# Seven products for eight in the second group's down projection, with weight sums made in two places

## The chip, the cores and the metric

One core of a Trainium2 chip runs the whole program. Its engines are TensorE (PE in the profile, with its weight loads as PEld), VectorE (DVE), ScalarE (ACT), GpSimd (POOL) and SyncE (SP), which here only issues transfers. The metric is the device time of one execution in microseconds; the kernel before took 1772.98 us (median of three runs, 1771.45 to 1773.77).

## The reference

A layer of an encoder, for 1024 tokens of a prompt and 32 tokens of a stream, 1056 in all. Of it this case touches the last part:

```python
h = x + jnp.einsum('bld,de->ble', m, w_out)
u = jnp.einsum('bld,df->blf', rmsnorm(h, g_ffn), w_up)
return h + jnp.einsum('blf,fd->bld', jnp.square(jax.nn.relu(u)), w_down)
```

`w_up` is 1024 x 4096, `w_down` 4096 x 1024. Ahead of it stand one input projection, sparse attention with an indexer, a stick-breaking attention and two gated branches.

## The kernel before, in words

**Numbers in two parts.** Each float32 operand of a product is split into a rounded part h (type fp32r) and the remainder l = x - h. A product is three matmuls, h·h, h·l and l·h (`three`). Splitting is a cast on ScalarE and a subtraction on VectorE or GpSimd.

**Groups and units.** Tokens run in two groups: group one is tokens 0 to 511, group two tokens 512 to 1055, as two halves ("chunks") of 272. Weights come as units: a 128x512 tile of DRAM holds four 128x128 blocks, of four row blocks and one column block. `unit` loads it into `wst` (three buffers), ScalarE casts it into `wh`, GpSimd writes `wl` (five pairs, `WB`). Four blocks times three matmuls are the 12 matmuls that a unit gives for one token chunk; they add up in one PSUM bank.

**The FFN.** `ffn_group` runs ups and downs for one group. An up (`go_up`) makes 128 rows of u for the group's tokens, then relu and square, split again into `mh`/`ml`, which hold 8 such rows. A down (`go_down(e, q)`) takes four of them and adds its product to column block e of y; there are 8 x 8 downs. The normalisation's factor, common to a token, is put on at the end (`acc`), and h is added, reloaded from DRAM into `g.h` (`reload`).

**Quads in group two.** Group two's ups work on two row blocks f, f+1 at a time (`go_up_quad`). Weights are seen as two by two blocks (the two row blocks, the two halves of the 1024 inputs), tokens as two halves, and the two by two product of such blocks is made with seven block products in place of eight, from sums of weights and sums of tokens. `quad_units` makes the weights' sums: SP loads one block into `raw`, and GpSimd issues transfers that add another block to it in SBUF. Sums' pairs are `sh`/`sl` (four pairs). The tokens' sums (`g.sums`) are made once, in `out` and `quarters`. Seven products of 12 matmuls are 84, where eight would be 96. Results come out of PSUM by copies (`part`), additions, `square` and the splits; some products add to a bank whose value up to then was copied out. Downs in group two are plain.

**The order of work.** The program records every operation with a rank and a cost by a formula (`Plan.record`, `cost`), and a planner issues, engine by engine, what it finds ready, of lowest rank first: FAST (reading out PSUM), PREP (weights), MAIN, FILL (matmuls), SLOW. All instructions are issued from one line, L410, so the profile is read by tile names. `behind` makes an SP transfer wait for the instruction recorded last. The planner also knows that GpSimd and some VectorE instructions exclude each other. Beside group one's FFN, the attention of the later tokens, those of group two, runs piece by piece (`late`).

Of the kernel before, what the change touches and what calls it, by code (L numbers as in the profile page):

```python
# [9 lines left out]
F32 = mybir.dt.float32  # L10
# [9 lines left out]
D = 1024  # L20
# [398 lines left out]
class Layer:  # L419
# [77 lines left out]
    def run(self):  # L497
# [34 lines left out]
        self.dh = dt([KB, 128, T], "dh")  # L532

# [104 lines left out]
        self.ffn_group(g2)  # L638
# [750 lines left out]
    def quad_units(self, f):  # L1389

        nc, a, w = self.nc, self.a, self.quads
        with nc.rank(PREP):
            src = lambda i, j: a["w_up"][f + i, j]

            def load(*blocks, out=None):
                st = out
                if out is None:
                    st = nc.tile(w, [128, 512], F32, "raw", bufs=10)
                    nc.sync.dma_start(st, src(*blocks[0]))
                    blocks = blocks[1:]  # L1400
                for b in blocks:
                    nc.gpsimd.dma_start(st, src(*b), accum_op=ALU.add)
                return st

            def part(z, pool, tag, bufs, eng):
                h = nc.tile(pool, [128, 512], F32R, tag + "h", bufs=bufs)
                l = nc.tile(pool, [128, 512], F32R, tag + "l", bufs=bufs)
                nc.scalar.copy(h, z)
                eng.tensor_sub(l, z, h.bitcast(F32))
                return h, l  # L1410

            V, G = nc.vector, nc.gpsimd
            z = load((1, 0), (1, 1))
            z3 = load((0, 0), (1, 0))
            a11, a22, a12 = load((0, 0)), load((1, 1)), load((0, 1))
            s1 = part(z, w, "s", 4, V)
            load((0, 0), out=z)
            s2 = part(z, w, "s", 4, V)
            load((0, 1), out=z)
            s3 = part(z3, w, "s", 4, V)  # L1420
            s4 = part(z, w, "s", 4, G)
            p11 = part(a11, self.wpool, "w", WB, G)
            p12 = part(a12, self.wpool, "w", WB, G)
            p22 = part(a22, self.wpool, "w", WB, G)
        return p11, p12, p22, s1, s2, s3, s4

    def square(self, g, ps, uh, ul, sign=1.0):

        nc = self.nc
        r = g.tmp("ru", "pb", 3)  # L1430
# [236 lines left out]
```

## Time and profile before

| | |
|---|---|
| median of the runs | 1772.98 us |
| profiled execution, its own time | 1771.3 us |
| its span in the profile | 1769.5 us |
| TensorE busy, matmuls | 98%, 11394 |
| VectorE, ScalarE, GpSimd busy | 59%, 55%, 59% |
| DMA | 264.53 MB, mean 149 GB/s |
| adding transfers (queue q0) | 16.78 MB |

Times in the profile count from the span's start. Matmuls are pipelined, and their records overlap, so their count in a stretch says more than their busy time. In the profile `pj` is a PSUM bank of an up or of group one, `pd` one of group two's downs; `xh`/`xl` and `gh`/`gl` are tokens or rows of u, `y` the result, `ru` a relu, `part` a copy out of PSUM. Group two's first matmul starts at 1293.59 us; its FFN fills the time from about 1400 us to the end.

### The profile page before, as it was taken

How to read it: one execution, taken by the hardware profiler on the slowest of the kernel's cores; microseconds unless marked ns; L12 is line 12 of the kernel's file. 1: busy time of each engine (PE TensorE's matmuls, PEld its weight loads, DVE VectorE, ACT ScalarE, POOL GpSimd, SP SyncE). 2: the span in 40 equal slices, each digit the busy share in tenths (PEclk: the TensorE clock that was granted, in tenths of full speed). 3: DMA queues.
4: the chain of work that ended last, by engine and by line, in shares of the span. 5: the costliest groups of instructions: out<-in, count | busy, mean ns of one | idle time of the engine just before them, and what ended most of it. 6: DMA issues, size and time to landing. Idle time of an engine off the chain costs nothing.

```text
span 1769.5 us, 32605 instructions
## 1 busy us (share of the span) xinstructions
PE 1741.2 (98%) x11394; PEld 1599.9 (90%) x11394; DVE 1050.6 (59%) x2284; ACT 976.5 (55%) x2153; POOL 1046.0 (59%) x909
## 2 busy tenths in 40 slices
PE   8999999999999999999999999999999999999999
PEld 7999999999889888988888888888899999999998
DVE  7555578999655644888755455222347843444445
ACT  7444598983255776766665555533236654444441
POOL 3623232435366575999864555665759966666555
PEclk9999999999999999999999999999999999999999
DMA  7243451444566668556344453533486576666634
GB/s 255 74 133 117 116 177 59 147 144 143 178 173 169 177 183 228 172 177 179 100 135 127 125 144 96 156 101 96 155 262 191 153 169 150 151 153 156 154 68 137
DMA packets 169908, 264.53 MB, mean 149 GB/s; under 512 B 28944, under 2 KB 58224, under 8 KB 169744
## 3 DMA queue, kind: packets, MB, share of 16 engines
q1 hardware_dynamic: 160096, 245.33, 47.3%
q0 software_dynamic: 9216, 16.78, 5.9%
q8 instruction: 90, 1.47, 0.4%
q14 instruction: 74, 0.61, 0.1%
q10 hardware_dynamic: 432, 0.34, 0.1%
HBM read 207.87 MB, written 54.40 MB: 148 GB/s over the span
## 4 chain that ended last, share of the span: by engine, by line
PE 85%; DMA 4%; POOL 4%; DVE 3%; issue 2%; ACT 1%; SPq 1%; ACTq 0%; POOLq 0%; DVEq 0%
PE pj L410 52%; PE s L410 13%; PE pd L410 11%; PE t L410 5%; PE o L410 5%; POOL wl L410 1%; DMA wst<-w_ba 1%; SPq L410 1%; DVE xl L410 1%; POOL xl L410 1%; POOL pb L410 1%; POOL acc L410 0%; DMA raw<-w_up 0%; DMA wst<-w_g 0%; DMA xt<-x 0%
## 5 line engine op out<-in xcount | busy, mean ns | idle before, releaser
L410 POOL TENSOR_TENSOR wl<-wst,wh 128x512 fp32r<-128x512 f32 x350 | 485.7, 1395 | 357.2 <-ACT wh L410 324.6
L410 PE MATMUL pj<-xh,wh 128*128 128x512 f32 (+1 forms) x1600 | 557.2, 349 | 0.7 <-DVE vt L410 0.3
L410 PE MATMUL pj<-xh,wl 128*128 128x512 f32 (+1 forms) x1600 | 557.5, 349 | 0.0
L410 PE MATMUL pj<-xl,wh 128*128 128x512 f32 (+1 forms) x1600 | 555.9, 348 | 0.1
L410 ACT CAST wh<-wst 128x512 fp32r<-128x512 f32 x350 | 216.9, 621 | 327.9 <-PE pj L410 167.4
L410 PEld LDWEIGHTS pj<-xh,wh 128*128 128x128 f32 x1600 | 300.8, 188 | 34.0 <-ACT xh L410 1.0
L410 PEld LDWEIGHTS pj<-xh,wl 128*128 128x128 f32 x1600 | 300.8, 188 | 32.9
L410 PEld LDWEIGHTS pj<-xl,wh 128*128 128x128 f32 x1600 | 301.0, 188 | 32.7 <-DVE xl L410 0.3
L410 PE MATMUL pd<-xh,wh 128*128 128x272 f32 x512 | 147.9, 289 | 2.1 <-ACT y L410 1.8
L410 PE MATMUL pd<-xl,wh 128*128 128x272 f32 x512 | 147.6, 288 | 0.0
L410 PE MATMUL pd<-xh,wl 128*128 128x272 f32 x512 | 147.6, 288 | 0.0
L410 DVE TENSOR_TENSOR tt<-t,tt 128x512 fp32r<-128x512 f32 (+2 forms) x168 | 100.5, 624 | 48.6 <-ACT tt L410 46.8
L410 DVE TENSOR_TENSOR_SCAN rem<-rem 128x896 f32<-128x896 f32 (+6 forms) x66 | 118.3, 1816 | 10.5 <-ACT rem L410 10.1
L410 ACT ACTIVATE junk<-score,cand 128x384 bf16<-128x384 f32 (+1 forms) x124 | 116.1, 936 | 9.8 <-DVE cand L410 7.8
L410 POOL TENSOR_TENSOR p<-p,rem 128x895 f32<-128x895 f32 (+6 forms) x66 | 100.9, 1541 | 30.3 <-DVE rem L410 25.3
L410 ACT CAST tt<-t 128x512 fp32r<-128x512 f32 (+2 forms) x168 | 84.6, 541 | 39.1 <-PE t L410 35.2
L410 PE MATMUL s<-wl,xh 128*128 128x256 f32 (+1 forms) x360 | 101.8, 286 | 0.2 <-POOL wl L410 0.2
L410 PEld LDWEIGHTS o<-tt,v 128*128 128x128 f32 x640 | 92.7, 188 | 9.5 <-ACT wh L410 0.8
L410 PE MATMUL s<-wh,xh 128*128 128x256 f32 (+1 forms) x360 | 100.3, 286 | 0.9 <-DVE small L410 0.8
L410 PE MATMUL s<-wh,xl 128*128 128x256 f32 (+1 forms) x360 | 100.8, 283 | 0.0
L410 PE MATMUL s<-k,q 128*128 128x384 f32 (+5 forms) x384 | 95.8, 356 | 4.7 <-DMA k<-dk 2.0
L410 PEld LDWEIGHTS pd<-xh,wh 128*128 128x128 f32 x512 | 96.5, 189 | 3.3 <-ACT y L410 2.0
(260 smaller groups left out, 3847.9 us busy)
## 6 DMA issues: line engine op xcount, KB each, us to landing
wst<-w_down SPq DMA_DIRECT2D x128, 256.0 KB, 2.7
raw<-w_up SPq DMA_DIRECT2D x80, 256.0 KB, 3.2
q<-dq SPq DMA_DIRECT2D x64, 256.0 KB, 5.2
wst<-w_up SPq DMA_DIRECT2D x64, 256.0 KB, 2.7
raw<-w_up POOLq DMA_DIRECT2D x64, 256.0 KB, 4.6
k<-dk SPq DMA_DIRECT2D x48, 256.0 KB, 3.5
v<-dv SPq DMA_DIRECT2D x48, 256.0 KB, 3.6
wst<-w_g SPq DMA_DIRECT2D x42, 256.0 KB, 3.4
```

The source lines that it names most:

```text
L410: fn(*args, **kw)
```

## The change

Group two gets an FFN of its own, `ffn_quads`. Ups pair row blocks four apart (f and f+4 of eight), and run four at a time: `up(q, j)` for j = 0 to 3 makes eight row blocks. With every result it keeps differences of the two token halves and of the two row blocks' results (`T1` to `T4`), split like the results. Then four `down(q, i)` take all of it and make, by seven products of 12 matmuls each, what two column blocks over eight row blocks add to y; there are four rounds (quarters) q.

The sums of `w_up` blocks that the ups need are made beforehand in DRAM, during group one's FFN: `weight_sums` is stepped by `tick`, once after an up and once in each round of downs, and for each quarter copies and adds transfers of 1 MB. The ups then load sums like any weights. The sums of `w_down` blocks are made on VectorE, from SBUF to SBUF, in `down_weights`. Both weights are laid out anew in DRAM so that blocks can be found. Loads use nine buffers in turn (`wst`, `raw`, `rb`, `sg`), pairs seven.

```diff
+    def weight_sums(self):
+        nc, a = self.nc, self.a
+        for (w, q), s in self.sums.items():
+            w11, w12, w21, w22 = (a[w][i, 4 * q:4 * q + 4].rearrange("t (a b) c -> (t a) (b c)", b=4) for i in range(4))
+            s1, s2, s3, s4 = s
+            def begin(out, src):
+                with nc.behind():
+                    nc.sync.dma_start(out, src)
+            def add(out, src):
+                nc.gpsimd.dma_start(out, src, accum_op=ALU.add, max_dma_last_dim=8192)
+            begin(s1, w21)
+            begin(s3, w11)
+            yield
+            add(s1, w22)
+            add(s3, w21)
+            yield
+            begin(s2, s1)
+            yield
+            add(s2, w11)
+            yield
+            begin(s4, s2)
+            yield
+            add(s4, w12)
+            yield
+    def tick(self):
+        with self.nc.rank(SLOW):
+            next(self.steps, None)
...
+    def ffn_quads(self, g):
...
+        def up_weights(q, j):
+            w11, w12, _, w22 = (a["w_up"][i, 4 * q + j] for i in range(4))
+            s1, s2, s3, s4 = (
+                z[32 * j:32 * j + 32].rearrange("a (b c) -> (a b) c", c=512) for z in self.sums["w_up", q])
+            for z, eng in zip((w11, s1, s2, s4, s3, w12, w22), (G, V, G, G, V, G, G)):
+                with nc.rank(PREP):
+                    wt = pair(load(z), eng)
+                yield wt
+        def down_weights(q, i):
+            src = [a["w_down"][p, 4 * q + i] for p in range(4)]
+            with nc.rank(PREP):
+                w11 = load(src[0])
+                wt = pair(w11, G)
+            yield wt
+            with nc.rank(PREP):
+                w21, w22 = load(src[2]), load(src[3])
+                z = turn("raw", raws)
+                add(z, w21, w22)
+                wt = pair(z, G)
+            yield wt
+            with nc.rank(PREP):
+                add(z, z, w11)
+                wt = pair(z, V)
+            yield wt
+            with nc.rank(PREP):
+                w12 = load(src[1])
+                add(z, z, w12)
+                wt = pair(z, G)
+            yield wt
+            for z, y, eng in ((w21, w11, V), (w12, None, G), (w22, None, V)):
+                with nc.rank(PREP):
+                    if y is not None:
+                        add(z, z, y)
+                    wt = pair(z, eng)
+                yield wt
...
+        def up(q, j):
...
+            product(next(wt), x[4], px)
+            pw = turn("bank", banks)
+            with nc.rank(FAST):
+                add(pw, px, p5)
+                square(pw, pw, -1.0)
+                parts(U22[j], pw, V)
+                sub(pz, pw, u12)
+                parts(T3[j], pz, V)
+            py = product(next(wt), x[5])
+            with nc.rank(FAST):
+                add(py, py, p1)
+                square(py, py, 1.0)
+                parts(U11[j], py, V)
+                sub(t1, py, u12)
+                parts(T1[j], t1, G)
+                V.scalar_tensor_tensor(t2, t1, -1.0, pw, op0=ALU.mult, op1=ALU.subtract)
+                parts(T2[j], t2, G)
+            product(next(wt), x[6], px)
+            with nc.rank(FAST):
+                square(px, px, -1.0)
+                parts(U21[j], px, V)
+                V.scalar_tensor_tensor(px, t2, -1.0, px, op0=ALU.mult, op1=ALU.subtract)
+                parts(T4[j], px, V)
+        def down(q, i):
...
+            px = product(next(wt), u[0])
+            gather(0, 0, px, 1.0, 0)
+            pz = product(next(wt), u[1])
+            gather(1, 1, pz, -1.0, 0)
+            product(next(wt), u[2], px)
+            gather(0, 1, px, 1.0, 0)
+            product(next(wt), u[3], pz)
+            gather(0, 1, pz, 1.0, 1)
+            product(next(wt), u[4], px)
+            gather(1, 1, px, -1.0, 1)
+            py = product(next(wt), u[5])
+            gather(0, 0, py, 1.0, 1)
+            product(next(wt), u[6], px)
+            gather(1, 0, px, -1.0, 2)
+        for q in range(4):
+            for j in range(4):
+                up(q, j)
+                if q + j == 0:
+                    self.scales(g)
+            if q == 3:
+                self.reload(g)
+            for i in range(4):
+                down(q, i)
...
     def ffn_group(self, g, late=iter(())):
...
             for f in range(4 * q + 1, min(4 * q + 5, 4 * nq)):
                 go_up(f)
+                if f >= 12:
+                    self.tick()
                 beside(2)
...
+                if q >= 3 and e == 3:
+                    self.tick()
                 beside(1)
```

The order moves with it. On GpSimd in FFN one, in the sixth of its eight rounds of downs, before has the remainders of weight units (`wl`) and squares (`ru`) alone:

```order
L410 TENSOR_TENSOR wl_8286<-wst_8284,wh_8285 128x512
L410 TENSOR_TENSOR ru_8267<-ru_8267 128x512
L410 TENSOR_TENSOR wl_8290<-wst_8288,wh_8289 128x512
L410 TENSOR_TENSOR wl_8294<-wst_8292,wh_8293 128x512
L410 TENSOR_TENSOR ru_8275<-ru_8275 128x512
L410 TENSOR_TENSOR wl_8298<-wst_8296,wh_8297 128x512
```

The changed kernel at the same units (numbers are 16 higher; `dw_up20` is the first sum of the third quarter, `dw_up13` the fourth sum of the second):

```order
L410 TENSOR_TENSOR wl_8302<-wst_8300,wh_8301 128x512
L410 TENSOR_TENSOR wl_8306<-wst_8304,wh_8305 128x512
L410 TENSOR_TENSOR ru_8291<-ru_8291 128x512
L410 DMA dw_up20_94<-w_up 128x2048
L410 DMA dw_up13_93<-w_up 128x2048
L410 TENSOR_TENSOR wl_8310<-wst_8308,wh_8309 128x512
L410 TENSOR_TENSOR wl_8314<-wst_8312,wh_8313 128x512
L410 DMA dw_up22_96<-w_up 128x2048
L410 TENSOR_TENSOR wl_8318<-wst_8316,wh_8317 128x512
```

Three adding transfers stand between remainders; each first waits for a copy. On SP the copies stand between the loads of the same units in the same way:

```order
L410 DMA wst_8304<-w_down 128x512
L410 DMA dw_up20_94<-w_up 16x16384
L410 DMA dw_up13_93<-dw_up11_91 16x16384
L410 DMA wst_8308<-w_down 128x512
L410 DMA wst_8312<-w_down 128x512
L410 DMA dw_up22_96<-w_up 16x16384
L410 DMA wst_8316<-w_down 128x512
L410 DMA wst_8320<-w_down 128x512
L410 DMA wst_8324<-w_up 128x512
L410 DMA wst_8327<-w_up 128x512
L410 DMA dw_up21_95<-dw_up20_94 16x16384
```

Before, SP has these loads alone. On VectorE in group two, before has for a round of downs one addition to y for every bank (`pd`), and a remainder of a sum (`sl`) before the next quad:

```order
L410 TENSOR_TENSOR y1_14401<-pd_16306,y1_14401 128x272
L410 TENSOR_TENSOR y1_14401<-pd_16307,y1_14401 128x272
L410 TENSOR_TENSOR y1_14401<-pd_16311,y1_14401 128x272
L410 TENSOR_TENSOR y1_14401<-pd_16312,y1_14401 128x272
L410 TENSOR_TENSOR y1_14401<-pd_16316,y1_14401 128x272
L410 TENSOR_TENSOR y1_14401<-pd_16317,y1_14401 128x272
L410 TENSOR_TENSOR sl_16374<-raw_16368,sh_16373 128x512
```

The changed kernel's downs of the second quarter:

```order
L410 TENSOR_TENSOR wl_16162<-rb_112,wh_16161 128x512
L410 TENSOR_TENSOR sl_16166<-wst_16156,sh_16165 128x512
L410 TENSOR_TENSOR y1_14457<-pj_16155,y1_14457 128x272
L410 TENSOR_TENSOR rb_112<-rb_112 128x512
L410 TENSOR_TENSOR wst_16178<-raw_16176,raw_16177 128x512
L410 TENSOR_TENSOR y1_14457<-y1_14457,pj_16133 128x272
L410 TENSOR_TENSOR y1_14457<-y1_14457,pj_16160 128x272
L410 TENSOR_TENSOR wl_16171<-raw_16157,wh_16170 128x512
L410 TENSOR_TENSOR y1_14457<-pj_16155,y1_14457 128x272
L410 TENSOR_TENSOR raw_16176<-raw_16176,raw_16172 128x512
L410 TENSOR_TENSOR wst_16178<-wst_16178,raw_16172 128x512
L410 TENSOR_TENSOR y1_14457<-pj_16160,y1_14457 128x272
```

Sums of 128x512 from SBUF (`rb`, `wst`, `raw`) and remainders now stand between the additions to y. On TensorE, where the second quarter turns from ups to downs, the first three down products (`pj_16133`, `pd_16139`, `pd_16149`) have run as far as the first three ups allow, and these are the first rows that need the fourth (`xh1`/`xl1` and `uh`/`ul` are the kept results and differences):

```order
L410 MATMUL pj_16133<-xh1_110,wh_16131 128x272
L410 MATMUL pd_16149<-uh_15798,sh_16147 128x272
L410 MATMUL pd_16139<-xh1_110,wh_16137 128x272
L410 MATMUL pj_16133<-xl1_111,wh_16131 128x272
L410 MATMUL pj_16133<-xh1_110,wl_16132 128x272
L410 MATMUL pd_16149<-ul_15799,sh_16147 128x272
L410 MATMUL pd_16149<-uh_15798,sl_16148 128x272
L410 MATMUL pd_16139<-xl1_111,wh_16137 128x272
L410 MATMUL pd_16139<-xh1_110,wl_16138 128x272
L410 MATMUL pj_16155<-xh1_110,wh_16153 128x272
```

Before has no such place: its downs take four rows of u of the round before, while the next ups run between them.

More of the change, by code (lines that the diff above doesn't have):

```diff
@@ L532, in run @@
         self.dh = dt([KB, 128, T], "dh")
+        self.sums = {(w, q): [dt([128, 2048], f"d{w}{q}{i}") for i in range(4)] for w in ("w_up",) for q in range(4)}
+        self.steps = self.weight_sums()
         self.wpool = nc.open("w")
@@ L1387, in quarters @@
             part(3, t4)
[L1389 to L1425, printed above, removed]
@@ new lines, in scales, with reload @@
+    def scales(self, g):
+        nc = self.nc
+        for c in range(len(g.chunks)):
+            ps = self.bank("pj")
+            nc.tensor.matmul(ps[:, :g.n], self.ones, g.acc[c], start=True, stop=True)
+            with nc.rank(FAST):
+                v = g.tmp("rv", "pb", 3)
+                nc.vector.tensor_scalar(v, ps[:, :g.n], 1.0 / D, EPS, op0=ALU.mult, op1=ALU.add)
+                nc.vector.reciprocal(g.acc[c], v)
+    def reload(self, g):
+        with self.nc.rank(PREP):
+            self.nc.sync.dma_start(
+                g.h.bitcast(F32), self.dh[:, :, g.lo:g.lo + g.w].rearrange("e p t -> p e t"))
@@ new lines, in up @@
+            px = product(next(wt), x[0])
+            keep(p1, px)
+            pz = product(next(wt), x[1])
+            keep(p5, pz)
+            product(next(wt), x[2], px)
+            keep(u2, px)
+            product(next(wt), x[3], pz)
+            with nc.rank(FAST):
+                add(pz, pz, u2)
+                square(u12, pz, 1.0)
+            product(next(wt), x[4], px)
[6 more added lines that the diff above has]
+                parts(T3[j], pz, V)
@@ new lines, in ffn_quads, with ffn_group, source, go_up @@
+        for q in range(4):
[3 more added lines that the diff above has]
+                    self.scales(g)
+            if q == 3:
+                self.reload(g)
+            for i in range(4):
+                down(q, i)
+    def ffn_group(self, g, late=iter(())):
+        nc, a = self.nc, self.a
+        nq, us = DFF // 512, {}
+        def source(name, row, col, t):
+            return a[name][2 * row + col, t]
+        def go_up(f):
+            units = [self.unit(source("w_up", f % 8 // 4, j, 4 * (f // 8) + f % 4)) for j in range(2)]
+            us[f] = uh, ul = g.mh[:, f % 8], g.ml[:, f % 8]
+            def done(c, cs, ps):
+                r = g.tmp("ru", "pb", 3)
+                nc.scalar.activation(r, ps, AF.Relu)
+                nc.gpsimd.tensor_mul(r, r, r)
+                nc.scalar.copy(uh[:, cs], r)
+                nc.vector.tensor_sub(ul[:, cs], r, uh.bitcast(F32)[:, cs])
+            self.column_block(units, lambda k, cs: (g.h[:, k, cs], g.l[:, k, cs]), done, g.chunks)
@@ L1511, in go_down @@
         def go_down(e, q):
-            units = [self.unit(a["w_down"][e, q])]
+            units = [self.unit(source("w_down", e % 2, q % 2, 4 * (q // 2) + e // 2))]
             def done(c, cs, ps):
@@ L1610, in _host_arrays @@
     out["w_ba"], out["w_bb"], out["w_out"] = units(f["w_branch_a"]), units(f["w_branch_b"]), units(f["w_out"])
-    out["w_up"], out["w_down"] = units(f["w_up"]), units(f["w_down"])
+    up, down = units(f["w_up"]), units(f["w_down"])
+    out["w_up"] = np.ascontiguousarray(
+        up.reshape(4, 2, 4, 2, 128, 512).transpose(1, 3, 0, 2, 4, 5).reshape(4, 16, 128, 512))
+    out["w_down"] = np.ascontiguousarray(
+        down.reshape(4, 2, 4, 2, 128, 512).transpose(1, 3, 2, 0, 4, 5).reshape(4, 16, 128, 512))
     out["g_mix"] = np.ascontiguousarray(f["g_mix"].reshape(KB, 128).T)
```

203 lines of the change are left out of this document (102 added, 101 removed).

## The prediction

> **What bounds the kernel now.** I read the page first: busy time by engine, the granted clock, and the chain that ended last.
>
> ```profile
> PE 1741.2 (98%) x11394; PEld 1599.9 (90%) x11394; DVE 1050.6 (59%) x2284; ACT 976.5 (55%) x2153; POOL 1046.0 (59%) x909
> PEclk9999999999999999999999999999999999999999
> PE 85%; DMA 4%; POOL 4%; DVE 3%; issue 2%; ACT 1%; SPq 1%; ACTq 0%; POOLq 0%; DVEq 0%
> ```
>
> TensorE is busy nearly throughout, at full clock, and 85% of the chain is its own. Busy matmuls overlap in the records, so I checked by stretches how densely they are issued (columns: PE, PEld, DVE, ACT, POOL busy with counts, clock, DMA share, GB/s).
>
> ```profile
> 1028.00:1275.00 247.00, 247.00 (x1202) 208.63 (x1202) 90.77 (x170) 105.43 (x191) 151.00 (x124) 1.00 0.43 126
> 1310.00:1330.00 20.00, 18.87 (x150) 18.65 (x150) 8.42 (x13) 9.73 (x17) 12.09 (x14) 1.00 0.99 283
> 1400.00:1410.00 10.00, 9.75 (x73) 9.18 (x73) 7.14 (x12) 5.55 (x15) 7.38 (x8) 1.00 0.53 149
> 1410.00:1420.00 10.00, 8.01 (x53) 7.79 (x52) 6.89 (x10) 4.23 (x10) 8.49 (x8) 0.84 0.79 159
> 1420.00:1430.00 10.00, 10.00 (x78) 9.70 (x77) 4.47 (x10) 4.83 (x12) 3.52 (x4) 0.99 0.60 129
> 1430.00:1440.00 10.00, 9.06 (x73) 8.84 (x71) 4.99 (x12) 5.45 (x14) 6.07 (x6) 1.00 0.90 191
> 1440.00:1450.00 10.00, 9.12 (x72) 9.12 (x73) 1.39 (x3) 6.64 (x17) 8.39 (x8) 1.00 0.70 168
> 1500.00:1700.00 200.00, 200.00 (x1597) 200.00 (x1596) 86.40 (x196) 90.02 (x196) 121.22 (x106) 1.00 0.63 143
> ```
>
> From 1500 to 1700, in group two's FFN, some 8 matmuls start per microsecond and nothing waits: that stretch is bound by the number of matmuls. Its price per matmul comes from the chain, whose pieces repeat once for each up quad with four downs (96 + 84 = 180 matmuls of 272 columns):
>
> ```profile
> 1537.27 8.92 PE pj L410 x71
> ...
> 1695.38 8.92 PE pj L410 x71
> ```
>
> Seven repeats in 158.11 us: 158.11 / (7 x 180) = 125.5 ns a matmul.
>
> **The matmuls removed.** Group two's downs are 8 x 8 column blocks x 2 token halves x 4 x 3 = 1536 matmuls; seven products for eight make 1344. The ups keep seven products (1344 matmuls). 192 x 125.5 ns = **-24.1 us**, if TensorE still sets the pace. The rest of the sum asks where it would not.
>
> **Side work in group two.** Durations, by form, from 1510 to 1690:
>
> ```profile
> L410 POOL TENSOR_TENSOR wl<-wst,wh 128x512 fp32r<-128x512 f32 x32 | 41.4, 1298 | 35.4 <-ACT wh L410 34.7
> L410 DVE TENSOR_TENSOR y<-pd,y 128x272 f32<-128x272 f32 x64 | 28.3, 442 | 45.1 <-PE pd L410 45.1
> L410 ACT CAST wh<-wst 128x512 fp32r<-128x512 f32 x32 | 19.9, 620 | 46.0 <-PE pd L410 35.8 <-PE pj L410 7.9 <-POOL wl L410 2.3
> L410 DVE TENSOR_TENSOR sl<-raw,sh 128x512 fp32r<-128x512 f32 x24 | 15.8, 686 | 23.8 <-ACT sh L410 23.8
> L410 DVE SCALAR_TENSOR_TENSOR pj<-pj,ru 128x272 f32<-128x272 f32 x32 | 14.2, 442 | 2.4 <-ACT ru L410 2.4
> L410 DVE TENSOR_TENSOR xl<-pj,xh 128x272 fp32r<-128x272 f32 x32 | 13.9, 434 | 3.3 <-ACT xh L410 3.3
> L410 ACT ACTIVATE ru<-pj 128x272 f32<-128x272 f32 x32 | 12.6, 394 | 13.4 <-DVE pj L410 13.4
> L410 ACT CAST xh<-pj 128x272 fp32r<-128x272 f32 x32 | 12.2, 380 | 0.0
> ```
>
> Either kind of unit is now 84 matmuls, 84 x 125.5 = 10.54 us; each other engine must stay below that.
> An up: ScalarE has 7 weight casts (0.620), 3 copies and 7 casts (0.380), 4 relus (0.394): 9.7 us. VectorE has 2 weight remainders (0.686) and 16 instructions of 272 columns (0.44): 8.4. GpSimd has 5 remainders (1.298) and 2 of 272 columns, at most 0.92 each: 8.3. All fit, ScalarE narrowly. Its 7 loads of 0.262 MB are 174 GB/s, an up and a down together (11) 137: below the 283 reached above, and near the 143 of 1500 to 1700.
> A down: ScalarE 7 x 0.620 = 4.3 (four more copies in the first quarter); GpSimd 4 x 1.298 = 5.2; VectorE 4 sums and 3 remainders of 128x512 from SBUF, 7 x 0.686 = 4.8, and 7 instructions that read out PSUM, 7 x 0.442 = 3.1, in all 7.9. In the last quarter the outputs are finished too: 14 in place of 7, 4.8 + 6.2 = **11.0 us, over 10.54**.
>
> These sums and remainders have two SBUF inputs, and such instructions take longer beside a busy GpSimd (by form, 1360 to 1400; the third row by group, 1150 to 1260):
>
> ```profile
> L410 DVE TENSOR_TENSOR raw<-raw 128x272 f32<-128x272 f32 x4 | 6.1, 1528 | 0.0
> L410 POOL TENSOR_TENSOR wl<-wst,wh 128x512 fp32r<-128x512 f32 x9 | 12.7, 1424 | 0.0
> L410 DVE TENSOR_TENSOR xl<-ru,xh 128x512 fp32r<-128x512 f32 x10 | 14.2, 1425 | 42.5 <-ACT xh L410 42.5
> ```
>
> Against 0.442 from PSUM, 272 columns from SBUF took 1.53; 512 columns took between 0.686 and 1.425. Bounds for one of the seven: 0.686 and 1.425. I take 0.78, near the row of the same stage, since GpSimd is wanted for 5.2 of 10.5 us there (in the 0.686 row's stretch for about 60%). Then the last four downs want 7 x 0.78 + 6.2 = 11.65, that is 4 x 1.1 = 4.4 us more than the matmuls; the other twelve, at 8.6, only read PSUM out late now and then. **+5 us** for the downs (0 to +53, below).
> The Trainium skill, SBUF — State Buffer, "Who interferes with whom", says that a VectorE instruction with two SBUF inputs and a GpSimd instruction that reads SBUF shut each other out for the whole of the first one. The trace agrees where GpSimd never rests (1.53 against 0.442); by that rule a down's 4.8 + 5.2 = 10.0 us would still go into 10.54.
>
> **Start and turns.** The five rows from 1400 to 1450 hold 349 matmuls where 50 / 0.1255 = 398 would fit: 6 us lost as group two's FFN starts. The worst stop:
>
> ```profile
> 1413.82 2.27 DVE L410 TENSOR_TENSOR sl<-raw,sh 128x512 fp32r<-128x512 f32 x1
> 1416.14 0.39 PE L410 MATMUL pj<-gh,sl 128*128 128x272 f32 x1 [1.99 <-DVE sl L410]
> ```
>
> A weight sum's remainder, behind GpSimd, holds TensorE for 2 us, and the clock of that 10 us row falls to 0.84. The changed kernel loads finished sums, with no adding transfer between two remainders; but its ups follow one another, so GpSimd has less room to catch up. Bounds -6 and +3; I take **-2**.
> The Trainium skill, TensorE: Matmul & The Clock Gate, "Why this matters for your kernels", asks for gaps of more than about 3 us before the clock falls. Here 2 us did it; by the page, the second rival below would cost 9 us instead of 15.
> At each of four turns from ups to downs, the first downs need the last up's differences. The order puts nine matmuls each of three down products ahead, then what needs the differences as it comes in; after the last up product 19 matmuls, 2.4 us, stand before its first use. The chain there is relu 0.394, multiply 0.442, cast 0.380, remainder 0.434 = 1.65 us and four handoffs. It fits closely: **+1** (0 to +15).
>
> **The sums' transfers in FFN one.** 16 copies and 16 adding transfers of 128x2048 float32, 1.05 MB each, 16.8 MB of either kind. In the order the first copy stands on SP behind the loads of the first row below, the last copy behind the reload of the second; so they run where before has 1028 to 1275. Prices are from 1500 to 1700:
>
> ```profile
> 1024.62 3.78 SPq L410 DMA_DIRECT2D wst<-w_down  x2
> 1266.59 0.38 SPq L410 DMA_DIRECT2D xh<-dh  x1
> ```
>
> ```profile
> q1 hardware_dynamic: 10821, 19.71, 35.8%
> q0 software_dynamic: 4768, 8.66, 27.0%
> ```
>
> Copies 0.358 x 200 / 19.71 = 3.6 us per MB, adds 0.27 x 200 / 8.66 = 6.2: 61 + 104 = 165 us of all engines. Free is (1 - 0.43) x 247 = 141: 24 us short. By the fastest row (283 GB/s at 0.99), 33.6 MB take 119 and fit. A transfer waits for the one before it, on SP for copies and on GpSimd for adds, and the weight loads, and remainders, of FFN one stand behind it. Their reserve:
>
> ```profile
> ACT wh L410 <- PE pj L410: 47.2, 23, 2.2
> ```
>
> ```profile
> 1195.04 19.31 SPq L410 DMA_DIRECT2D wst<-w_up  x8
> ```
>
> Casts wait for TensorE to free a buffer (1150 to 1260), so all five pairs are full; a unit lasts (19.31 - 0.33) / 7 = 2.7 us, and four pairs ahead, less cast and remainder (1.9), are 8.9 us. So the shortage costs 0 to 15 us. I take **+2**: the new rows are four times as long as those priced.
> Before, GpSimd issued 64 adding transfers in group two; those go, with no gain on TensorE's path.
>
> **Sum.** 1769.5 - 24.1 + 5 - 2 + 1 + 2 = 1751.4 us of span. The profiled execution took 1771.3, 1.8 over its span, and the median 1772.98 is 1.7 over that: 1751.4 + 3.5 = **1755 us**.
>
> **Rivals.**
> *The sums' transfers saturate* (0.14): 24 us short less 8.9 reserve = 15 in place of 2: 1768. For it, 165 against 141; against it, 119.
> *The turns stall* (0.10): the remainder comes 2.3 us late as at 1413.82, with 0.16 x 10 = 1.6 us of lost clock, four times: 15 in place of 1: 1769. Against it, the order's fill.
> *VectorE and GpSimd bind the downs*, slower (0.09): at 1.425 us for each of the seven, a down is 10.0 + 3.1 = 13.1 us, 2.5 over, twelve times, and in the last quarter 16.2, 5.6 over, four times: 30 + 23 = 53 in place of 5: 1803. It decides once the seven average 1.15 us, where the excess (12 x 0.6 + 4 x 3.7 = 22) eats the matmuls saved. For it, the 1.425 row; against it, 0.686 in the same stage.
> *All hidden, the start mended* (0.05): 1769.5 - 24.1 - 6 + 3.5 = 1743.
> That the change doesn't do what it says is excluded: the order has 192 matmuls fewer.
>
> **Chances and range.** The forecast has 0.62, with 1746 to 1763 of its own. The range 1746 to 1770 takes in the first two rivals and leaves out the third and fourth with a little of each tail. The measurement tells 0.2%, 3.5 us, from no change. Faster (below 1769.4): 0.62 + 0.05 + nearly all of 0.14 + half of 0.10 = 0.84; within: 0.08; slower: 0.08.
>
> **What would show it.** Right: 192 fewer matmuls; 125 ns each in the middle of group two; FFN one still at 1202 matmuls in its 247 us. Wrong: TensorE waiting for `wl` in FFN one, with a DMA share near 1 (transfers); waits for VectorE's `ul` or `xl` once per 84 us (turns); VectorE near 100% in the downs with 128x512 sums above 1.1 us (port). The forecast falls if any of these costs over 10 us, or if group one's part before 1028 moves.

## The result, and the profile after

The changed kernel took 1784.9 us (median of seven runs, 1781.0 to 1796.3), the kernel before 1771.45 beside it (seven runs; the 1772.98 above is of three): 1.0088 times as long, 95% interval 1.0071 to 1.0105. It is slower, by 13 us by the medians and 16 by the ratio; 1755 was forecast, and the range ended at 1770. Its runs also lie farther apart than those of before (15 us against 3.4), and the profiled execution, 1796.3, is the slowest of them. So a single stage of it is compared below with the same stage of other kernels.

The page of the changed kernel, busy time, clock and the chain that ended last:

```profile
PE 1740.3 (97%) x11202; PEld 1586.7 (88%) x11202; DVE 1164.0 (65%) x2448; ACT 1015.4 (57%) x2249; POOL 1070.5 (60%) x901
PEclk9999999999999999999999999999999999999999
PE 78%; DMA 8%; DVE 7%; POOL 2%; issue 2%; ACT 1%; SPq 0%; POOLq 0%; DVEq 0%; ACTq 0%
```

192 matmuls are gone (11394 to 11202), but TensorE's share of the chain fell from 85% to 78%, and what came in is DMA (4% to 8%) and VectorE (3% to 7%). The program falls into three stages by places that every kernel here has: the start, VectorE's first remainder `xl<-ru,xh` of FFN one, TensorE's first 272-column matmul of group two, and the end. The stages hold the same work in all of them but a_first, a_all, a_mix and a_mixh, where FFN one has 7 to 88 matmuls more and the stage ahead of it as many fewer. Read from the instructions' starts (us):

| kernel | to FFN one | FFN one | group two | span |
|---|---|---|---|---|
| before | 858.1 | 435.5 | 475.9 | 1769.5 |
| changed | 866.6 | 465.6 | 462.3 | 1794.5 |
| difference | +8.5 | +30.1 | -13.6 | +25.0 |

**FFN one.** The stretch by windows, first of before, then of the changed kernel (PE, PEld, DVE, ACT, POOL busy with counts, clock, DMA share, GB/s):

```profile
1028.00:1180.00 152.00, 152.00 (x783) 129.99 (x783) 65.37 (x143) 74.17 (x138) 90.84 (x75) 1.00 0.45 130
1180.00:1293.00 113.00, 113.00 (x500) 93.55 (x499) 37.69 (x44) 35.62 (x61) 74.47 (x60) 1.00 0.43 130
```

```profile
1028.00:1180.00 152.00, 148.44 (x769) 126.59 (x768) 66.22 (x160) 76.78 (x140) 95.72 (x80) 1.00 0.70 196
1180.00:1293.00 113.00, 102.67 (x420) 80.85 (x419) 20.35 (x24) 28.90 (x50) 59.64 (x52) 0.95 0.90 248
```

From 1180 on 420 matmuls run where 500 did, at a DMA share of 0.90 and a clock of 0.95. The DMA view of 1150 to 1293, before and then changed (queues: packets, MB, share; issues: count, size, median us to landing):

```profile
q1 hardware_dynamic: 9529, 17.56, 40.7%
wst<-w_down SPq DMA_DIRECT2D x25, 256.0 KB, 2.6
wst<-w_up SPq DMA_DIRECT2D x22, 256.0 KB, 2.6
```

```profile
q1 hardware_dynamic: 6958, 23.13, 45.8%
q0 software_dynamic: 1440, 10.49, 37.9%
dw_up<-w_up POOLq DMA_DIRECT2D x11, 1024.0 KB, 12.5
wst<-w_up SPq DMA_DIRECT2D x22, 256.0 KB, 6.5
wst<-w_down SPq DMA_DIRECT2D x21, 256.0 KB, 4.4
```

A weight load that landed in 2.6 us now takes 4.4 to 6.5. In 1150 to 1335, ScalarE's casts, which used to wait for TensorE, wait for the loads:

```profile
ACT wh L410 <- DMA wst<-w_down: 48.8, 9, 10.7
ACT wh L410 <- DMA wst<-w_up: 32.9, 12, 6.1
```

**Group two.** Two windows, the first without a turn, the second around the third quarter's turn from ups to downs:

```profile
1598.00:1640.00 42.00, 42.00 (x336) 42.00 (x336) 25.45 (x54) 25.44 (x58) 26.33 (x22) 1.00 0.56 164
1640.00:1664.00 24.00, 22.62 (x170) 21.47 (x169) 22.84 (x46) 17.02 (x42) 17.37 (x14) 1.00 0.28 82
```

Between turns 8 matmuls start per microsecond, as before. At the turn it is 170 where 191 would fit at 125.5 ns each, 2.7 us lost, and VectorE is busy for 22.84 of 24 us. The chain in the turn's last 7 us runs through VectorE alone (start, length, what):

```profile
1655.82 0.59 DVE wl L410
1656.41 0.36 DVE pd L410
1656.77 1.35 DVE wst L410
...
1661.26 1.03 DVE sl L410
1662.29 0.35 DVE pj L410
1662.64 0.35 DVE y L410
1663.00 0.04 issue
1663.04 9.07 PE pj L410 x70
```

The last up's differences stand in VectorE's queue behind sums (`wst`) and remainders (`wl`, `sl`) of the first downs' weights, and these are long. By form, 1500 to 1780:

```profile
L410 DVE TENSOR_TENSOR wl<-raw,wh 128x512 fp32r<-128x512 f32 x16 | 16.0, 998 | 9.0 <-ACT wh L410 8.8
L410 DVE TENSOR_TENSOR wst<-wst,raw 128x512 f32<-128x512 f32 x10 | 12.1, 1209 | 2.0 <-POOL wl L410 2.0
L410 DVE TENSOR_TENSOR raw<-raw 128x512 f32<-128x512 f32 x9 | 10.4, 1153 | 0.0
```

Over all 138 of the 128x512 kind from 1437 to 1782 the mean is 1.04 us, where I took 0.78.

### The profile page after: what moved, and what is told of

The parts are those of the page before. It is cut to its first block, busy times and chain, and to the rows that moved or that the text cites. A ratio compares the mean times of both kernels' runs of the same rounds, so it can differ in the third digit from the quotient of the medians.

```text
span 1794.5 us, 32622 instructions
## 1 busy us (share of the span) xinstructions
PE 1740.3 (97%) x11202; PEld 1586.7 (88%) x11202; DVE 1164.0 (65%) x2448; ACT 1015.4 (57%) x2249; POOL 1070.5 (60%) x901
## 4 chain that ended last, share of the span: by engine, by line
PE 78%; DMA 8%; DVE 7%; POOL 2%; issue 2%; ACT 1%; SPq 0%; POOLq 0%; DVEq 0%; ACTq 0%
PE pj L410 53%; PE s L410 13%; PE t L410 5%; PE o L410 4%; DMA wst<-w_up 4%; PE pd L410 2%; POOL wl L410 1%; DMA wst<-w_down 1%; DVE pj L410 1%; DMA q<-dq 1%; DVE xl L410 1%; ACT wh L410 1%; DVE wst L410 0%; DVE raw L410 0%; DMA k<-dk 0%
## 5 line engine op out<-in xcount | busy, mean ns | idle before, releaser
L410 PE MATMUL pj<-xh,wh 128*128 128x512 f32 (+1 forms) x1864 | 640.5, 344 | 15.6 <-ACT wh L410 7.1
L410 PE MATMUL pj<-xh,wl 128*128 128x512 f32 (+1 forms) x1864 | 639.7, 344 | 5.2 <-POOL wl L410 5.1
L410 PE MATMUL pj<-xl,wh 128*128 128x512 f32 (+1 forms) x1864 | 636.5, 342 | 0.7 <-DVE xl L410 0.7
L410 PEld LDWEIGHTS pj<-xh,wh 128*128 128x128 f32 x1864 | 354.4, 190 | 54.5 <-ACT wh L410 10.3
L410 PEld LDWEIGHTS pj<-xh,wl 128*128 128x128 f32 x1864 | 353.8, 190 | 42.1 <-POOL wl L410 8.8
L410 PEld LDWEIGHTS pj<-xl,wh 128*128 128x128 f32 x1864 | 354.2, 190 | 34.0 <-DVE xl L410 1.2
L410 DVE TENSOR_TENSOR y<-pj,y 128x512 f32<-128x512 f32 (+1 forms) x95 | 55.5, 584 | 88.7 <-PE pj L410 88.5
L410 PE MATMUL o<-tt,v 128*128 128x256 f32 (+1 forms) x640 | 99.6, 279 | 0.4 <-ACT wh L410 0.4
L410 PE MATMUL t<-ident,p 128*128 128x128 f32 x596 | 90.4, 276 | 2.5 <-POOL p L410 2.5
L410 DVE TENSOR_TENSOR xl<-ru,xh 128x512 fp32r<-128x512 f32 x32 | 36.1, 1127 | 84.0 <-ACT xh L410 83.9
```

The costliest lines, as they stand in the source:

```text
L410: fn(*args, **kw)
```

## The experiments

Eighteen kernels beside the two. The ratio is to the kernel before, run beside them (its medians lay between 1768.3 and 1770.5). The stages are those of the table above, from one profiled execution each.

| kernel | ratio (interval) | to FFN one | FFN one | group two |
|---|---|---|---|---|
| b_sums | 1.0149 (1.0134-1.0164) | 858.1 | 463.1 | 477.7 |
| b_copies | 1.0004 (0.9993-1.0014) | 861.7 | 436.8 | 474.2 |
| a_nosums | 0.9914 (0.9901-0.9927) | 860.3 | 435.5 | 458.0 |
| a_noadds | 0.9975 (0.9960-0.9989) | 857.9 | 459.3 | 447.3 |
| a_norem | 1.0036 (1.0023-1.0049) | 857.5 | 458.2 | 454.0 |
| a_shift | 1.0052 (1.0035-1.0068) | 861.0 | 459.5 | 462.1 |
| a_half | 1.0053 (1.0038-1.0068) | 857.9 | 455.8 | 460.9 |
| a_early | 1.0068 (1.0043-1.0093) | 861.4 | 458.9 | 462.3 |
| a_first | 1.0179 (1.0164-1.0194) | 888.0 | 447.6 | 462.0 |
| a_all | 1.0248 (1.0226-1.0271) | 913.1 | 446.5 | 447.5 |
| a_r5 | 1.0010 (0.9994-1.0027) | 859.8 | 449.5 | 461.2 |
| a_both | 1.0001 (0.9986-1.0016) | 857.5 | 447.4 | 457.0 |
| a_late | 1.0033 (1.0019-1.0048) | 857.1 | 438.3 | 478.2 |
| a_best | 1.0075 (1.0055-1.0095) | 855.9 | 437.2 | 485.0 |
| a_p2k | 1.0056 (1.0035-1.0076) | 861.1 | 455.9 | 461.3 |
| a_p2kr5 | 1.0030 (1.0016-1.0044) | 859.3 | 452.5 | 460.7 |
| a_mix | 1.0130 (1.0116-1.0145) | 893.3 | 438.4 | 460.3 |
| a_mixh | 1.0133 (1.0108-1.0158) | 893.8 | 437.7 | 461.4 |

Two readings of the table itself. Up to FFN one, kernels with the same program there stand at 855.9 to 861.7, so the changed kernel's +8.5 is that execution's own and not the change's. In FFN one, five kernels with the same transfers and buffers (changed, a_shift, a_noadds, a_norem, a_half) took 455.8 to 465.6: that stage varies by 10 us from one execution to the next, and with it the time. Group two repeats within 2 us (460.3 to 462.3 where its program is the same; a_nosums, whose ups load other blocks, has 458.0).

### The transfers, and the sums on VectorE, apart

b_sums is the kernel before with `weight_sums` and its ticks, at the same places:

```diff
                 go_up(f)
+                if f >= 12:
+                    self.tick()
                 beside(2)
...
+                if q >= 3 and e == 3:
+                    self.tick()
                 beside(1)
```

> The kernel before, plus the 16 copies and 16 adding transfers of the changed kernel at the same places of group one's FFN; nothing uses the sums. Theory one (the transfers take the weight loads' turn in the last 170 us of FFN one, where 12 of 16 adds stand): 15 to 28 us more than before, 1787 to 1800, and group two's first 272-column matmul 15 to 30 us later than 1293.6. Rival (the loss has another source: the new layout of DRAM, or the planner's other order): within 4 us of before, as the prediction's +2 had it.

a_nosums is the reverse:

```diff
-        self.steps = self.weight_sums()
+        self.steps = iter(())
...
-            s1, s2, s3, s4 = (
-                z[32 * j:32 * j + 32].rearrange("a (b c) -> (a b) c", c=512) for z in self.sums["w_up", q])
+            s1, s2, s3, s4 = (a["w_up"][i, 4 * q + j] for i in (2, 0, 1, 3))
```

> The changed kernel without the 32 transfers of the sums: the ups load plain blocks of w_up in their place, so u is computed from other weights, by the same number of loads, casts and matmuls. Theory one: 15 to 28 us less than the changed kernel, 1757 to 1770, and FFN one ends as before. Rival (another source): still 1780 to 1790. With theory one and nothing lost elsewhere it would be the prediction less 2, 1753; what it stands above that is the turns'.

The transfers alone added 1.49%, 26 us, to the kernel before; without them the changed kernel is at 0.9914, 31 us below its 1.0088, and FFN one takes 435.5 us, as before. Theory one holds by both: the transfers cost 26 to 31 us, nearly all in FFN one. The window of b_sums reads like that of the changed kernel:

```profile
1180.00:1293.00 113.00, 102.82 (x420) 80.56 (x419) 23.93 (x25) 30.28 (x53) 64.06 (x55) 0.95 0.89 249
```

a_noadds takes VectorE's four sums out of each down:

```diff
-                z = turn("raw", raws)
-                add(z, w21, w22)
-                wt = pair(z, G)
+                wt = pair(w21, G)
...
-                add(z, z, w11)
-                wt = pair(z, V)
+                wt = pair(w22, V)
... (so for the other two)
```

> The changed kernel without the four sums of w_down that VectorE makes for each down: the products take the plain blocks instead, so y is another sum, with the same loads, casts, remainders and matmuls. Theory two (VectorE, with seven two-input instructions of 1.06 us mean in place of 0.78, is behind where ups turn to downs, 13 us in four turns): 8 to 13 us less than the changed kernel, 1772 to 1777. Rival (the turns wait for the last up's own chain of relu, multiply, cast and remainder): within 3 us of the changed kernel.

a_norem leaves VectorE's work and takes GpSimd's:

```diff
+            if eng is None:
+                return h, last[0]
             eng.tensor_sub(l, st, h.bitcast(F32))
+            if eng is V:
+                last[0] = l
...
-                wt = pair(w11, G)
+                wt = pair(w11, None)
... (so for all four G of down_weights)
```

> The changed kernel without GpSimd's four remainders in each down: those products use VectorE's last remainder in their place, so y has wrong low parts; VectorE's instructions stay as they are, all of them. If the two-input instructions are slow because GpSimd holds what both read SBUF through: they fall from 1.06 to 0.6-0.7 us in the downs, and the time falls by 8 to 13 us, to 1772 to 1777, as without the sums. If they are slow by themselves: 1.06 stays, and the time too, 1782 to 1788.

Without the sums group two took 447.3 us, 15.0 less, and the turns' stops are gone (a window around a turn):

```profile
1620.00:1640.00 20.00, 19.83 (x157) 19.47 (x156) 16.07 (x38) 14.62 (x36) 13.81 (x13) 1.00 0.43 131
```

That is 157 matmuls where 159 would fit at 125.5 ns, with VectorE at 16 of 20 us. So the turns waited for VectorE's backlog, not for the last up's own chain. In a_norem, without GpSimd's remainders of the downs, VectorE made all its sums and remainders, and each was shorter (1500 to 1755):

```profile
L410 DVE TENSOR_TENSOR wl<-raw,wh 128x512 fp32r<-128x512 f32 x15 | 11.9, 795 | 8.5 <-ACT wh L410 5.4 <-DMA raw<-w_up 3.1
L410 DVE TENSOR_TENSOR wst<-wst,raw 128x512 f32<-128x512 f32 x8 | 5.5, 684 | 0.0
L410 DVE TENSOR_TENSOR raw<-raw 128x512 f32<-128x512 f32 x7 | 5.4, 767 | 0.0
```

The two kinds of sum shown before fall from 1.15 and 1.21 us to 0.77 and 0.68 (all 128x512 ones: 1.04 to 0.76), and group two gains 8.3 of the 15.0. That TensorE no longer needs GpSimd's remainders is not what gained it: in group two's FFN TensorE waited for GpSimd for 1.7 us in the changed kernel and for 2.2 in a_norem. More than half of what VectorE's sums cost is thus the two engines' standing in each other's way; the rest is their number. The Trainium skill, SBUF — State Buffer, "Who interferes with whom", has GpSimd's reads and VectorE's two-input instructions shut each other out; these rows agree, 1.21 us beside GpSimd's remainders of the downs and 0.68 without them.

a_shift gives VectorE fewer remainders and GpSimd more:

```diff
-            for z, y, eng in ((w21, w11, V), (w12, None, G), (w22, None, V)):
+            for z, y, eng in ((w21, w11, G), (w12, None, G), (w22, None, G)):
```

> The changed kernel with two more of each down's remainders on GpSimd (six) and one left on VectorE beside its four sums. If VectorE's own load decides: 5 x 1.06 + 3.1 = 8.4 us a down, and the time falls by 5 to 10 us, 1775 to 1780. If the time in which the two engines exclude each other decides: what is left of VectorE's instructions grows longer beside GpSimd's 6 x 1.42 us, and the time is within 3 us of the changed kernel's, or longer.

Its group two takes 462.1 us, as before the edit, and the sums left on VectorE grew longer:

```profile
L410 DVE TENSOR_TENSOR wst<-wst,raw 128x512 f32<-128x512 f32 x8 | 9.9, 1237 | 0.0
L410 DVE TENSOR_TENSOR raw<-raw 128x512 f32<-128x512 f32 x7 | 8.9, 1276 | 0.3 <-POOL wl L410 0.3
```

The second reading of its expectation holds: moving such work between the two engines moves nothing. The ratio, 1.0052 for 1.0088, comes from the start and FFN one (861.0 and 459.5 us), where nothing was edited.

a_half makes two of a down's four sums by adding transfers into SBUF:

```diff
-                w21, w22 = load(src[2]), load(src[3])
-                z = turn("raw", raws)
-                add(z, w21, w22)
+                z = load(src[2])
+                G.dma_start(z, src[3], accum_op=ALU.add)
                 wt = pair(z, G)
... (w21 + w11 in the same way)
```

> The changed kernel with two of each down's four sums (w21 + w22 and w21 + w11) made by adding transfers into SBUF, 32 in all, and two left on VectorE. By theory two VectorE has 5 x 1.0 + 3.1 = 8.1 us a down in place of 10.5, and 10 to 15 of the 18.6 us go that the kernel without sums gained: 1769 to 1775. If the adding transfers come too late for the products: within 4 us of the changed kernel, with waits for them at TensorE.

Group two gained 1.4 us, not 10, though VectorE has two instructions fewer in each down; a down also loads five blocks for four now, beside its two adding transfers. TensorE waits for other things (1420 to 1770):

```profile
PE pj L410 <- DVE wl L410: 2.7, 2, 2.3
PE pd L410 <- ACT wh L410: 2.2, 2, 2.0
PE pj L410 <- ACT ut L410: 2.1, 3, 1.2
```

The first two are remainders and casts of weights that came late, the third is a copy of a result. That these waits are what ate the gain is likely, but no run takes them away.

### Why the transfers cost 26 us: place, buffers, kind, pieces

a_early ticks from the third up on; a_first puts two steps behind each projection and gate of the first 450 us; a_all does so too, and goes on through FFN one with w_down's sums, so that VectorE makes none:

```diff
-                if f >= 12:
+                if f >= 2:
                     self.tick()
```

```diff
             self.project_b(p)
+            self.tick()
+            self.tick()
```

```diff
-for w in ("w_up",) for q in range(4)}
+for w in ("w_up", "w_down") for q in range(4)}
...
+            for z, eng in zip((w11, s1, s2, s4, s3, w12, w22), (G, G, V, G, V, G, V)):
+                with nc.rank(PREP):
+                    wt = pair(load(z), eng)
```

> The changed kernel with its transfers one step after each up of FFN one from the third up on, not from the thirteenth: the same 32 transfers, begun some 170 us earlier, most of them beside the attention of group two's tokens, where before has a DMA share of 0.23 to 0.5. Theory one a (they cost because they bunch where FFN one runs alone and takes a weight unit every 2.7 us): most of the 26 us goes, 1758 to 1768. Theory one b (each transfer of a megabyte holds up what is queued behind it, wherever it stands): 20 us or more stay, 1778 to 1788.

> The same 32 transfers, two steps after each projection and gate of the first 450 us, where before has a DMA share of 0.2 to 0.6 and weights are wanted more seldom. Theory one a: 1754 to 1762, near the kernel without the transfers (1755.6). Theory one b: 20 us or more over that, lost before 450 us.

> Both w_up's sums and w_down's by transfers, 64 in all: w_up's in the first 450 us, w_down's from there to the end of FFN one; VectorE makes no sums, and each down loads seven blocks in place of four. Theories one a and two together: the 29 us of the transfers and most of the 18 us of VectorE's sums go, 1738 to 1750. Against: the transfers of w_down beside FFN one cost 5 to 15 of it again (1750 to 1762); one b: above 1775.

None paid. In a_early 825 matmuls run from 860 to 1028 where before has 934, at a share of 0.70:

```profile
860.00:1028.00 168.00, 155.52 (x825) 133.85 (x825) 84.85 (x162) 89.24 (x173) 103.33 (x76) 0.95 0.70 197
975.00:995.00 20.00, 9.39 (x51) 7.64 (x49) 6.60 (x19) 5.19 (x10) 6.26 (x6) 0.80 1.04 244
```

Of TensorE's two longest stops there, 5.7 and 4.9 us, the second is a wait for a load of the attention's own (`q`). The second row shows what the average of 0.70 hides: adding transfers are under way up to 990, the share is 1.04 (packets count where they start, so it can pass 1), and 51 matmuls run where before has 114. a_first lost 42 us, 30 of it by the table before FFN one. The 12 that the table has in FFN one are work that the planner moved there: that stage holds 2315 matmuls for 2227 in before, and TensorE's waits in it come to 0.2 us. That the transfers bunch in FFN one is then not the whole cause: stretches that are free by their averaged share have no room while an adding transfer is under way. a_all's group two, 447.5 us, is that of a_noadds: with w_down's sums made elsewhere it is short, but the 64 transfers cost 66 us before group two (55.0 and 11.0), where a_first's 32 cost 42.

a_r5 lets loads in FFN one use two halves of the tile `rb` beside `wst`'s three buffers; a_both adds a_half's edit:

```diff
+            self.loads += 1
+            i = self.loads % 5 - 3
+            if self.wide and i >= 0:
+                st = self.rb[:, 512 * i:512 * i + 512]
+            else:
                 st = nc.tile(self.wpool, [128, 512], F32, "wst", bufs=3)
```

> The changed kernel with five buffers for weight loads in FFN one in place of three (the two more are halves of a tile that FFN one leaves idle); transfers and sums as they are. With three buffers a load may take about 3 x 2.7 us less cast and remainder (1.9), some 6.2 us, before TensorE waits; with five some 11.7. Theory (the loads' longer way beside the transfers, 5.2 to 6.5 us median in FFN one's last 170 us for 2.6 before, is what TensorE waits for): 10 to 22 us less than the changed kernel's ratio, 1762 to 1774. Rival (the 16 DMA engines are full, and no reserve helps what lasts 150 us): within 6 us, 1778 to 1786.

> Both edits: the sum of what each of the two gains, 1748 to 1762, below the kernel before (1769) if either theory holds in full; near the better of the two if the same time is counted twice.

Five buffers brought the ratio to 1.0010, 14 us less, and FFN one to 449.5 us, though its loads landed no sooner (1150 to 1293):

```profile
q0 software_dynamic: 1584, 11.54, 40.9%
wst<-w_up SPq DMA_DIRECT2D x14, 256.0 KB, 7.5
wst<-w_down SPq DMA_DIRECT2D x13, 256.0 KB, 7.0
```

So half of the transfers' price was the loads' longer way through three buffers: at one unit per 2.7 us, three bear 3 x 2.7 - 1.9 = 6.2 us by this estimate, and the loads of `w_up` took 6.5. Some 14 us in FFN one stayed. a_both, 1.0001, equals the kernel before and no more.

What stayed was still open, and the copies were set apart from the adding transfers: b_copies drops the adds of b_sums, and a_late moves half of all steps into group two.

```diff
             def add(out, src):
-                nc.gpsimd.dma_start(out, src, accum_op=ALU.add, max_dma_last_dim=8192)
+                return
```

```diff
-                if f >= 12:
+                if f >= 12 and f % 3 == 0:
                     self.tick()
...
-        for _ in self.steps:
-            pass
... (a tick after each up and down of ffn_quads)
```

> The kernel before with the 16 copies alone, without the 16 adding transfers. By their time on the engines (copies 3.0 us a megabyte, adding transfers 5.2): 16.8 x 3.0 = 50 of 138 us, and a cost of 9 of the 26 us or less, 1769 to 1778. If what counts is that loads queue behind copies, which use the same queue as the loads while the adding transfers have one of their own: 15 us or more, 1784 and up.

> The changed kernel with the transfers of quarters zero and one in FFN one, spread over the same stretch, and those of quarters two and three in group two's FFN, one step after each up and down of its first two quarters. If full DMA engines are the price: FFN one, with 8 of 16 adding transfers, loses 5 to 12 us in place of 22 to 28, group two has room (share 0.3 to 0.6, nine buffers), and the time is 10 to 18 us less than the changed kernel's, 1767 to 1775. If each transfer has its price wherever it stands: within 4 us of the changed kernel.

> The transfers spread so, five load buffers in FFN one, and two of each down's four sums by adding transfers. If full engines are the price: below the 1.000 of the two edits without the spreading by 5 to 10 us, 1758 to 1765, faster than before by 0.3 to 0.6%. If not, or if the adding transfers of the downs and those of w_up get into each other's way in group two: 1768 to 1776.

The copies cost nothing that can be measured (1.0004); loads beside them land in 2.6 to 2.8 us, though they share a queue. Their window, and that of a_late with 5 adding transfers in place of 11:

```profile
1180.00:1293.00 113.00, 113.00 (x500) 93.62 (x499) 35.71 (x41) 36.99 (x64) 76.29 (x62) 1.00 0.58 198
```

```profile
1180.00:1293.00 113.00, 113.00 (x500) 93.55 (x500) 36.81 (x44) 35.15 (x60) 75.94 (x63) 1.00 0.65 191
```

Both keep TensorE's 500 matmuls; at 0.89 and above it is 420 to 456. The prices follow: adding transfers 0.379 x 143 / 10.49 = 5.2 us of all engines per MB, copies, from b_copies' queue row less that of before, 2.3:

```profile
q1 hardware_dynamic: 9727, 27.96, 57.7%
```

(0.577 - 0.407) x 143 / (27.96 - 17.56) = 2.3. The changed kernel issued 12 adds and 12 copies of 1.05 MB from 1148 on: 65 + 29 = 94 us, where before leaves (1 - 0.41) x 143 = 84 free. Ten are short, near the 14 that a_r5 still lost. With a_late's half it fits.

These runs leave one rival of the engines' time. b_copies takes out the adds, and with them the waits for them: a copy that waits for an add holds SP, with the weight loads behind it, and an add that waits for a copy holds GpSimd, with the remainders behind it. From 1150 to 1335 SP stood 11.1 us for adds in the changed kernel and 22.8 in a_r5, GpSimd 7.7 and 15.5 us for transfers of the sums; in a_late, which has few adds there, it was nothing and 0.3. In b_sums two such transfers lie on the chain one behind the other:

```profile
1185.37 8.80 DMA dw_up<-w_up
1194.16 0.02 issue
1194.18 6.44 DMA dw_up<-dw_up
```

How much of the 14 us is the engines' time, and how much this order, no run tells.

Group two, where a_late's other half went, lost 16 us (478.2 for 462.3), and a_best, with the downs' adding transfers there too, 28 against a_both (485.0 for 457.0). What holds them up there is open.

The last four kernels asked whether adding transfers can be had cheaper: a_p2k in pieces of 2048 bytes (in the packet records a piece of 8192 holds an engine for 629 ns, a load's piece of 2048 for 84), a_p2kr5 with five buffers too; a_mix with one step, not two, per projection and gate of the first 450 us (10 adds), the other 6 spread over FFN one, and five buffers; a_mixh with a_half's edit too.

```diff
-                nc.gpsimd.dma_start(out, src, accum_op=ALU.add, max_dma_last_dim=8192)
+                nc.gpsimd.dma_start(out, src, accum_op=ALU.add, max_dma_last_dim=2048)
```

```diff
             self.project_b(p)
+            self.tick()
...
-                if f >= 12:
+                if f >= 12 and f % 3 == 0:
                     self.tick()
```

> The changed kernel with the sums' adding transfers in pieces of 2048 bytes in place of 8192; nothing else. A load has 8 pieces for each engine. If an engine takes a piece from each queue in turn, a load beside an adding transfer takes 8 x (84 + 178) ns = 2.1 us of it in place of 8 x (84 + 629) = 5.7 us: loads land in 3 to 4.5 us in FFN one's last 170 us (5.2 to 6.5 before), and 12 to 22 us of the transfers' 26 go, 1763 to 1774. If the bytes count and not the pieces: within 4 us of the changed kernel.

> The same with five load buffers in FFN one. If the pieces decide: 1756 to 1766, faster than before by 0.2 to 0.8%, and near the kernel without transfers (1755.6). If the bytes count: as with the five buffers alone, 1768 to 1774.

> The changed kernel with one step of transfers after each projection and gate of the first 450 us (10 adding transfers), the other 6 spread over FFN one, and five load buffers there. If what counts is how many adding transfers stand in a stretch: the early ones cost 0 to 6 us, FFN one 0 to 3, and the time is 1756 to 1764, faster than before by 0.3 to 0.7%. If each has its price of 1 to 1.6 us wherever it stands: 1772 to 1780.

> The same, and two of each down's four sums by adding transfers into SBUF. Alone that edit took 6 us off the changed kernel: 1750 to 1758 if the early transfers are cheap, 1766 to 1774 if not.

The size of the pieces is not the cause, or at most a small part of it: loads still took 6.1 to 6.8 us at a share of 0.97, the interval of a_p2k's ratio touches that of the changed kernel (1.0076 and 1.0071 are their near ends), and with five buffers the small pieces gained nothing. Thin transfers at the beginning cost as much as dense ones, 35 us for 10. In the two longest stops of TensorE there, what comes late is not a weight load but a store that lies on the path. Two places of a_mix's chain, and its windows around them:

```profile
152.31 13.49 DMA dk<-zz
...
167.53 2.40 PE s L410 x6
```

```profile
374.55 16.81 DMA dq<-az
...
392.80 1.12 PE t L410 x4
```

```profile
152.00:166.00 14.00, 11.36 (x65) 9.95 (x64) 4.42 (x8) 4.10 (x10) 4.19 (x4) 0.98 1.01 254
374.00:391.00 17.00, 11.30 (x83) 10.48 (x81) 9.26 (x32) 8.60 (x18) 3.33 (x4) 0.99 0.96 227
```

A store of 256 KB, 3.3 us by the median of its kind in before, took 13.5, and one of 16 KB, 1.9 us in before, 16.8. Both fell beside adding transfers, and in both windows the DMA engines are full (1.01 and 0.96; before has 0.51 and 0.24 there). TensorE stood for 4.2 and 7.2 us. Of the kernels that compute the same, none is faster than the kernel before; the best is a_both, at no difference.

## Why the prediction was wrong, point by point

- **The matmuls, -24.1**: right. 192 fewer, at the same 8 per microsecond between turns. With the sums out of VectorE's way (a_noadds) group two is 28.6 us shorter than before, and 24.1 at this price are most of it.
- **The start, -2**: right in sign. From 1395 to 1450 TensorE's waits come to 4.5 us in before (2.0, 1.8 and 0.7) and to 3.2 in the changed kernel (1.7, 0.9 and 0.6). The rest of what a_noadds gained beyond the matmuls has no run of its own.
- **The sums' transfers, +2**: the step that failed most; b_sums measured 26. My own sum had the transfers 24 us short and the cost between 0 and 15. I took 2 since the new rows are four times as long as those priced, and since the fastest row had the 33.6 MB fit into 119 us. That row is of another mix: 4.44 MB of plain transfers at 65.8% and only 1.19 MB of adding ones at 33.0%. By its own two prices, 3.0 and 5.5 us a megabyte, 16.8 MB of either kind take 143 us, for 141 free. The free time was also counted over too long a stretch, the 247 us from 1028 to 1275. By the prices measured (2.3 for copies, where I had 3.6, and 5.2 for adds, where I had 6.2) 126 us are needed there and 141 are free, so by this sum nothing would be lost. But ticks come with ups, and ups come slowly while the attention runs beside them: 12 of 16 adding transfers were issued from 1176 on, in the last 156 us of the stage. For the last 143 us of before's stage the sum has 94 needed and 84 free. Last, the reserve was taken as 8.9 us to be used up once; a load that is longer all the time is borne only up to what three buffers hold, 6.2 us by the estimate above, and two buffers more gained 14 us. The rival with its 15 us was right in place and in kind, and too small: its 15 is about what stayed with five buffers, which is luck.
- **The downs, +5, and the turns, +1**: together 15.0 measured, as group two's difference to a_noadds. The step at fault is 0.78 us for the instructions with two SBUF inputs; the mean was 1.04, and the two commonest kinds of sum took 1.15 and 1.21. I chose the value near one end since GpSimd has pauses in the downs; a_norem showed that 0.76 is what they take without GpSimd's remainders of the downs, so the pauses were worth next to nothing. VectorE's own work is then 7 x 1.04 + 3.1 = 10.4 us of a down's 10.54, and what it is behind shows where ups become downs, not in the last quarter. The turns' own chain, the +1, held: in a_noadds TensorE's waits for VectorE's `ul` come to 0.5 us. The rival of the turns had the size (15) and the place, but by another mechanism; the rival of the port had the mechanism, at a smaller price, since 1.04 stayed under its 1.15.
- **Both at once**: the rivals were priced one at a time. Each was known to draw on a cause of its own, DMA in FFN one and VectorE in group two; both came, 1769.5 - 13.6 + 27.6 = 1783.5 by the stages of the changed kernel and of b_sums, near the 1781.4 that the changed median less 3.5 gives. The range ended where one alone would have put the time.
- **What the text asked to look at**: waits for `wl` in FFN one came with a share near 1, and group one's part before 1028 stayed, but for one execution's 8.5 us. VectorE is near full at the turns.
- **The clock**: I wrote that 2 us of stop brought it down. In the changed kernel a stop of 2.8 us ends at 1223 and the granted clock is 0.50 from 1226 to 1228; stops of 1.2 and 0.5 us end at 1482.6 and 1483.5, and it is 0.51 from 1486 to 1488. The Trainium skill, TensorE: Matmul & The Clock Gate, "Why this matters for your kernels", puts it at about 3 us; these rows differ, and they decide.

## What to carry to other kernels

A resource's free time must be counted in the stretch in which the new work will run, not over the stage: read from the order which events trigger it, and how dense these are in time. An averaged share of 0.45 or 0.70 is no room either: read it over a stretch as long as one transfer takes, for here it stood near 1 in each of the three short windows shown, where TensorE waited beside adding transfers. What late transfers cost then depends on how many buffers stand between them and TensorE. A price is taken from a row with the same mix of transfers. And when two rivals have causes of their own, give their joint case a price and a chance.

## What was not expected of the hardware

Copies of 1.05 MB, in the weight loads' own queue, left the loads at 2.6 to 2.8 us and the time where it was; adding transfers of the same size, in another queue, took them to 6.5 and cost 26 us, for 2.2 times the copies' time on the engines (the part of it that is order in the queues is not known). A 16 KB store beside one took 16.8 us, with the engines at 0.96. Between VectorE and GpSimd, a sum of 128x512 took 0.68 us without GpSimd's remainders of the downs and 1.21 beside them, and moving remainders from one engine to the other (a_shift) lengthened the sums to 1.24 to 1.28 and left group two's time as it was. Why so small a store waits until the adding transfers are through is left open; the size of their pieces made little difference to the weight loads.
